# Eight more gate blocks in the mLSTM stage, between its heads, and two operations moved from POOL and DVE to ACT

## The chip, the cores and the metric

The kernel runs on one core of one Trainium2 chip. The metric is the device time of one execution in microseconds, the median over several runs. The engines are PE (matrix products), DVE (VectorE), ACT (ScalarE), POOL (GpSimd) and SP, which here only issues DMAs.

## The reference

One layer of a hybrid block over 512 latent tokens of width 1024 and 256 context tokens: a modulated norm, one wide projection, three branches (RWKV-7 with 8 heads, a depthwise convolution, mLSTM with 4 heads), a gated merge, and an MLP. Cut to what matters here:

```
h = rmsnorm(x, g_norm1) * (1 + mod_x[1]) + mod_x[0]
u_rw, u_cv, u_ml, u_gate = split(h @ w_in)        # u_gate: 3 x 1024 columns
ya = rwkv7(u_rw, context)                         # two directions, a scan over tokens
yc = mlstm(u_ml, context)                         # two directions, 4 heads
   hn = layernorm(h, nw);  return hn * sigmoid(o)
yb = silu(layernorm(depthwise_conv(a * sigmoid(g))))
ga, gb, gc = split(sigmoid(u_gate))
m = ga * (ya @ pa) + gb * (yb @ pb) + gc * (yc @ pc)
x = x + mod_x[2] * (m @ wo)
x = x + mod_x[5] * (square(relu(h2 @ w1)) @ w2);  return rmsnorm(x, g_final)
```

## The kernel before

All tokens stay on one core, features on the 128 partitions. Matrix products keep fp32 precision by splitting each operand into a high and a low part: a product of a 128 x 512 weight half takes three PE products (high by high, high by low, low by high). Each weight half is loaded by SP into `raw` (256 KB), ACT writes its high part `whi`, POOL its low part `wlo` (`whalf`, lines 156 to 160). A **dense block** of 128 output features takes two halves and 24 products of 128 x 128 by 128 x 512; its result lies in one of two PSUM banks (tag "d").

The stages, by time in the span: features of RWKV up to 300 us; the **mLSTM stage** from 300 to 531; four **weaves** of the RWKV scan, 531 to 620, 620 to 707, 707 to 793 and 793 to 870; the rest of the projections and the modulation vectors up to 948; then the merge and the MLP up to the end.

The mLSTM stage. `front(h)` computes a head's key, value, query and output gate by dense blocks (line 293), transposes them, and runs the state over its chunks: per chunk the key block is weighted on POOL into `kw` (line 836), PE multiplies it (`st`, line 838). `back(h)` computes the output: products `psc` and `acc`, a norm on DVE, four transposes into `pt` (line 889), and DVE's product into `yc` (line 891), stored to DRAM (line 892). Between the heads, DVE computes the convolution's taps (line 324), and the first RWKV pair's matrices are prepared: Gram products `pg` on PE (line 1006), a triangular inversion on DVE by rows (`N` and `tmp`, lines 1045 to 1052, `TN` 1055 and 1057), and its products `px` (lines 1066 to 1082). Last come the stage's gate blocks: dense products `dl`, tanh on ACT into `gt` (line 524), a store (line 525).

A weave runs one pair's scan: `chain` has 12 chunks of three steps each, S (line 1133), X (1139) and V (1148, with DVE's `SV`, 1149), where each step waits for ACT or DVE behind the step before. Between the steps, other work is issued: the next pair's matrices (`nxt`), and products of one stream `dense_`: gate blocks that the mLSTM stage left over (`gates()`, products `dg`, line 545), then the projections of two branches (`projections()`, products `dp`, line 624), which read the gates back (`ld`, line 619). `DENSE[j]` says how many products of the stream are paced evenly over the 36 steps of weave j, `EXTRA[j]` how many follow them. Weave 3 has in place of `nxt` the norm of the convolution branch (`conv_norm`) and the modulation sums (`wad` loads, DVE `accm`, line 641). What is left of the stream runs after the weaves.

The program is written in this order, and a scheduler places each instruction on its engine by its priority and modelled readiness; on the chip, each engine runs its list in order. A tile's tag and its number of buffers (`bufs`) say which earlier tile has to be done with.

Of the kernel before, what the change touches and what calls it, by code (L numbers as in the profile page):

```python
# [7 lines left out]
F32 = mybir.dt.float32  # L8
# [3 lines left out]
AF = mybir.ActivationFunctionType  # L12
# [5 lines left out]
P = 128  # L18
# [37 lines left out]
NRAW, NHI = 3, 4  # L56
NGA = 6
PART = (2, 4)
# [18 lines left out]
def build(tc, wblk, wada, xin, cin, params, lora, consts, rowp, out, dbg=None):  # L77
# [426 lines left out]
    for i, z, y in tiles:  # L504
        SY.dma_start(z, sp["z", i][:, :])
    st[0] = front(0)
    st[1] = front(1)
    back(0, *st[0])
    taps(tiles)
    for i, z, y in tiles:  # L510
# [3 lines left out]
    rw.open_a()  # L514
    rw.run(rw.ctx(0), rw.lat(0))
    st[2] = front(2)
    back(1, *st[1])
    st[3] = front(3)
    back(2, *st[2])
    back(3, *st[3])  # L520
    for g in range(NGA):
        ps, = dense(B_GA + g)
        t = SM.tile([P, NT], F32, tag="qT", name="gt", bufs=2)
        A.activation(t[:, :], ps[:, :], AF.Tanh, scale=0.5)
        SY.dma_start(sp["g", g][:, :], t[:, :])
    emm.close()
# [192 lines left out]
def mlstm(tc, nc, S, SG, PS1, dense, CN, C, ident, nwh, epsc, sp, sp_rows, dump, consts):  # L719
# [76 lines left out]
    def front(h):  # L796
# [13 lines left out]
        A.activation(to[:, :], pl[:, :], AF.Tanh, scale=0.5)  # L810
        G.tensor_scalar(to[:, :], to[:, :], 1.0, None, ALU.add)

# [11 lines left out]
        for d in range(2):  # L824
# [8 lines left out]
            for p in range(5):  # L833
                c = orders[d][p]
                kw = S.tile([P, 128], F32, tag="kw", name="kw", bufs=2)
                G.tensor_scalar(kw[:, :], ktok[:, c, :], cols[:, c, 2, rr:rr + 1], None, ALU.mult)
                st = PS1.tile([P, 129], F32, tag="tp", name="st", bufs=2)
                PE.matmul(st[:, :], lhsT=kw[:, :], rhs=v1[:, c, :], start=True, stop=True)
                if p == 0:
                    V.tensor_copy(cs[:, 0, :], st[:, :])  # L840
                else:
                    V.scalar_tensor_tensor(cs[:, p, :], cs[:, p - 1, :], wib[:, c * 128 + last:c * 128 + last + 1],
                                           st[:, :], ALU.mult, ALU.add)
# [3 lines left out]
    def back(h, qT, kT, to, v1, qs, Cst):  # L847
# [42 lines left out]
        yc = S.tile([P, NT], F32, tag="yc", name="yc")  # L890
        V.scalar_tensor_tensor(yc[:, :], pt[:, :], nwh[:, h:h + 1], to[:, :], ALU.mult, ALU.mult)
        SY.dma_start(sp["yc", h][:, :], yc[:, :])
# [4 lines left out]
PACE = [4] * 8 + [3] * 8 + [2] * 12 + [0] * 8  # L897
DENSE = (100, 100, 100, 110)
EXTRA = (20, 20, 20, 20)

# [621 lines left out]
```

## Time and profile before

| | |
|---|---|
| median of 3 runs | 1376.44 us (1365.84 to 1383.73) |
| profiled execution, its own time | 1368.34 us |
| its span | 1366.6 us |
| busy: PE | 1238.3 us (91%) |
| busy: DVE, ACT, POOL | 858.2, 511.2, 583.0 us |
| mean granted clock of PE | 0.955 |

Times in the rows are microseconds from the start of the span; ns where marked. A row of the windows gives the window, its length, then for PE, PEld (weight load), DVE, ACT and POOL the busy time with the number of instructions, then the granted clock of PE as a share of full speed, the busy share of the DMA engines, and GB/s. A row of a timeline gives start, length, engine, line, operation, output<-input, shapes, and in brackets the idle time before with what ended it. A row of the groups gives count, busy time, mean ns, and idle time before with its releasers. The chain of waits follows the work that ended last in a window back, and shares it out by line. Where many products follow each other, the distance of their starts tells their pace; their lengths overlap.

### The profile page before, as it was taken

Reading aid. Unit: us, or ns where it says so; the run is one execution under the profiler, and the core shown is the slowest. Engines: PE = TensorE matmul, PEld = TensorE weight load, DVE = VectorE, ACT = ScalarE, POOL = GpSimd, SP = SyncE. Lnnn points to the kernel's source line nnn. Section 1 sums busy time; section 2 is a strip of 40 time slices with the busy share of each in tenths; the row PEclk is TensorE's granted clock in tenths of the full one; section 3 lists DMA queues with packets and bytes.
Section 4 is the critical chain, followed back from the end, with each engine's and each line's share of the span. In section 5 each row is a group of like instructions: output and inputs, shape, how many; then the busy total and the mean of one; then the engine's idle time right before and its main releaser. Section 6 shows DMA issues by size and latency. Waiting matters only on the chain.

```text
span 1366.6 us, 21733 instructions
## 1 busy us (share of the span) xinstructions
PE 1238.3 (91%) x8020; PEld 964.7 (71%) x8020; DVE 858.2 (63%) x1513; ACT 511.2 (37%) x1048; POOL 583.0 (43%) x547
## 2 busy tenths in 40 slices
PE   5989989776999886998998888989999999999997
PEld 2678867565888675666676555667887878888886
DVE  5698788798357984796978957688284533300202
ACT  4426567432222221342443445322364333322222
POOL 1633434329554523332433454433465544444542
PEclk9999999888999998998999998999999999999999
DMA  9312688722622315241431254876444422432332
GB/s 375 99 58 63 197 264 245 229 75 70 200 78 91 125 53 150 85 131 60 136 117 48 86 164 146 275 247 234 139 131 142 136 93 93 154 101 95 129 98 87
DMA packets 101457, 187.85 MB, mean 137 GB/s; under 512 B 10708, under 2 KB 29396, under 8 KB 100328
## 3 DMA queue, kind: packets, MB, share of 16 engines
q1 hardware_dynamic: 101352, 186.47, 43.0%
q8 instruction: 63, 1.03, 0.3%
q14 instruction: 42, 0.34, 0.1%
HBM read 148.64 MB, written 29.40 MB: 130 GB/s over the span
## 4 chain that ended last, share of the span: by engine, by line
PE 42%; DVE 17%; DMA 6%; issue 2%; ACT 1%; POOL 0%; SPq 0%; DVEq 0%; ACTq 0%; POOLq 0%
PE pt L1301 16%; PE pd L1370 13%; DMA wad<-wada 5%; PE dg L545 4%; DVE N L1052 3%; DVE tmp L1050 3%; PE pg L1006 2%; DVE N L1045 2%; DVE accm L641 1%; PE pd L715 1%; DVE LT L1075 1%; PE ch L1133 1%; DVE SV L1149 1%; PE dl L293 1%; PE ch L1139 1%
## 5 line engine op out<-in xcount | busy, mean ns | idle before, releaser
L160 POOL TENSOR_TENSOR wlo<-raw,whi 128x512 fp32r<-128x512 f32 x296 | 430.8, 1461 | 554.8 <-ACT whi L159 496.3
L159 ACT CAST whi<-raw 128x512 fp32r<-128x512 f32 x296 | 181.7, 619 | 322.0 <-PE pt L1301 114.1
L293 PE MATMUL dl<-hh,whi 128*128 128x512 f32 (+1 forms) x344 | 143.2, 416 | 5.2 <-ACT kT L791 4.3
L293 PE MATMUL dl<-hh,wlo 128*128 128x512 f32 (+1 forms) x344 | 140.5, 408 | 0.0
L293 PE MATMUL dl<-hl,whi 128*128 128x512 f32 (+1 forms) x344 | 139.7, 406 | 0.0
L1370 PE MATMUL pd<-h2h,wlo 128*128 128x512 f32 (+1 forms) x272 | 105.2, 388 | 0.0
L1370 PE MATMUL pd<-h2l,whi 128*128 128x512 f32 (+1 forms) x272 | 104.5, 386 | 0.6 <-POOL h2l L1353 0.6
L1396 DVE TENSOR_TENSOR x<-pt,modb 128x512 f32<-128x512 f32 x8 | 5.5, 691 | 154.8 <-PE pt L1301 154.8
L1370 PE MATMUL pd<-h2h,whi 128*128 128x512 f32 (+1 forms) x272 | 102.3, 383 | 0.2 <-ACT h2h L1350 0.2
L1301 PE MATMUL pt<-whi,h1l 128*128 128x512 f32 x256 | 99.7, 389 | 0.0
L1301 PE MATMUL pt<-whi,h1h 128*128 128x512 f32 x256 | 99.7, 389 | 0.0
L1301 PE MATMUL pt<-wlo,h1h 128*128 128x512 f32 x256 | 99.2, 389 | 0.0
L293 PEld LDWEIGHTS dl<-hh,whi 128*128 128x128 f32 (+1 forms) x344 | 66.9, 194 | 20.4 <-ACT kT L791 4.5
L1374 DVE TENSOR_TENSOR relu<-relu 128x512 f32<-128x512 f32 x32 | 43.7, 1367 | 57.9 <-ACT relu L1373 57.8
L641 DVE SCALAR_TENSOR_TENSOR accm<-wad,scz,accm 128x512 f32<-128x512 f32 x56 | 57.6, 1028 | 34.2 <-DMA wad<-wada 33.6
L293 PEld LDWEIGHTS dl<-hh,wlo 128*128 128x128 f32 (+1 forms) x344 | 66.8, 194 | 14.3 <-issue 0.4
L293 PEld LDWEIGHTS dl<-hl,whi 128*128 128x128 f32 (+1 forms) x344 | 66.6, 194 | 13.8 <-issue 1.3
L1146 POOL TENSOR_TENSOR sps<-SV,PL 64x128 f32<-64x128 f32 x88 | 40.0, 454 | 78.6 <-DVE SV L1149 75.5
L545 PE MATMUL dg<-hl,whi 128*128 128x512 f32 x144 | 65.8, 457 | 0.0
L545 PE MATMUL dg<-hh,whi 128*128 128x512 f32 x144 | 65.0, 451 | 0.0
L545 PE MATMUL dg<-hh,wlo 128*128 128x512 f32 x144 | 64.9, 450 | 0.0
L1370 PEld LDWEIGHTS pd<-h2l,whi 128*128 128x128 f32 x272 | 51.7, 190 | 12.5 <-POOL h2l L1353 0.9
(399 smaller groups left out, 2824.7 us busy)
## 6 DMA issues: line engine op xcount, KB each, us to landing
raw<-wblk SPq DMA_DIRECT2D x296, 256.0 KB, 2.9
wad<-wada SPq DMA_DIRECT2D x64, 256.0 KB, 4.1
wada<-wada SPq DMA_DIRECT2D x8, 1024.0 KB, 12.0
BK<-kb SPq DMA_DIRECT2D x16, 384.0 KB, 5.1
sp_bk<-BK SPq DMA_DIRECT2D x8, 768.0 KB, 5.5
BK<-sp_bk SPq DMA_DIRECT2D x8, 768.0 KB, 4.2
sp_g<-gt SPq DMA_DIRECT2D x24, 256.0 KB, 2.0
sp_al<-al SPq DMA_DIRECT2D x8, 640.0 KB, 5.2
```

The source lines that it names most:

```text
L159: A.copy(hi[:, :], raw[:, :])
L160: G.tensor_tensor(lo[:, :], raw[:, :], hi[:, :], ALU.subtract)
L293: PE.matmul(ps_[0:M, :], lhsT=w[:, ko:ko + M], rhs=x[seg][:, k, :], start=(n == 0), stop=(n == 3 * KT - 1))
L545: yield lambda w=w, x=x, k=k, ko=ko, n=n: PE.matmul(ps[:, :], lhsT=w[:, ko:ko + P], rhs=x[:, k, :], start=(n == 0), stop=(n == 3 * KT - 1))
L641: V.scalar_tensor_tensor(o, t[:, :], sc[:, k, 0:1], o, ALU.mult, ALU.add)
L1006: PE.matmul(ps[hf, i, :, :], lhsT=BK[dd, c, x, :], rhs=al[:, c] if lat else AL[d][dd, 8 + c:9 + c, :], start=True, stop=True)
L1050: V.tensor_tensor(tv, N[:, s + 1:32, s:s + 1].to_broadcast([P, n, s]), N[:, s:s + 1, 0:s].to_broadcast([P, n, s]), ALU.mult)
L1052: V.tensor_tensor(N[:, s + 1:32, 0:s], N[:, s + 1:32, 0:s], tv, ALU.add)
L1146: last["Pool"] = G.tensor_tensor(sps[hf], SV[d][hf, c, :, :], PL[hf, c, :].unsqueeze(2).to_broadcast([64, 2, CH]), ALU.mult)
L1301: PE.matmul(pss[i][:, :], lhsT=x[:, k, ts_], rhs=w[:, :], start=(k == 0 and n == 0), stop=(k == nk - 1 and n == 2))
L1370: PE.matmul(ps[:, ts_], lhsT=w[:, ko:ko + P], rhs=x[:, k, ts_], start=(k == 0 and n == 0), stop=(k == 7 and n == 2))
L1374: V.tensor_tensor(t[:, :], t[:, :], t[:, :], ALU.mult)
```

## The change

Fourteen in place of six gate blocks are computed in the mLSTM stage, by calls of `gate(n)` between its heads, and what the weaves take of the stream falls from 120 to 64 products each in weaves 0 to 2, and rises from 130 to 140 in weave 3. The gate's result `gt` moves from two buffers of tag "qT" to the single buffer of tag "yc", which it shares with the heads' output. The key weighting `kw` goes from POOL to ACT; the output gate `to` is scaled and shifted on ACT, so that the last product of a head is a plain product on DVE.

```diff
--- before.py
+++ after.py
@@ -54,7 +54,7 @@
     _o += _c
 NCONST = _o
 NRAW, NHI = 3, 4
-NGA = 6
+NGA = 14
 PART = (2, 4)
 
 
@@ -503,9 +503,22 @@
     tiles = [(i, CZ.tile([P, 752], F32, name=f"cz{i}")[:, :], CZ.tile([P, NT], F32, name=f"cy{i}")[:, :]) for i in (2, 3)]
     for i, z, y in tiles:
         SY.dma_start(z, sp["z", i][:, :])
+
+    left = iter(range(NGA))
+
+    def gate(n):
+        for _, g in zip(range(n), left):
+            ps, = dense(B_GA + g)
+            t = SM.tile([P, NT], F32, tag="yc", name="gt")
+            A.activation(t[:, :], ps[:, :], AF.Tanh, scale=0.5)
+            SY.dma_start(sp["g", g][:, :], t[:, :])
+
     st[0] = front(0)
+    gate(1)
     st[1] = front(1)
+    gate(1)
     back(0, *st[0])
+    gate(2)
     taps(tiles)
     for i, z, y in tiles:
         SY.dma_start(sp["yb", i][:, :], y)
@@ -513,16 +526,17 @@
     rw = Rwkv(tc, CN, C, ident, epsc, PL, sp, dump)
     rw.open_a()
     rw.run(rw.ctx(0), rw.lat(0))
+    gate(1)
     st[2] = front(2)
+    gate(2)
     back(1, *st[1])
+    gate(1)
     st[3] = front(3)
+    gate(2)
     back(2, *st[2])
+    gate(1)
     back(3, *st[3])
-    for g in range(NGA):
-        ps, = dense(B_GA + g)
-        t = SM.tile([P, NT], F32, tag="qT", name="gt", bufs=2)
-        A.activation(t[:, :], ps[:, :], AF.Tanh, scale=0.5)
-        SY.dma_start(sp["g", g][:, :], t[:, :])
+    gate(NGA)
     emm.close()
     ew.close()
     ehc.close()
@@ -808,7 +822,7 @@
         to = S.tile([P, NT], F32, tag="to", name="to", bufs=2)
         pl, = dense(B_ML + 12 + h)
         A.activation(to[:, :], pl[:, :], AF.Tanh, scale=0.5)
-        G.tensor_scalar(to[:, :], to[:, :], 1.0, None, ALU.add)
+        A.activation(to[:, :], to[:, :], AF.Identity, scale=nwh[:, h:h + 1], bias=nwh[:, h:h + 1])
 
         v1 = S.tile([P, 6, 129], F32, tag="v1", name="v1", bufs=2)
         G.memset(v1[:, :, 128:129], 1.0)
@@ -833,7 +847,7 @@
             for p in range(5):
                 c = orders[d][p]
                 kw = S.tile([P, 128], F32, tag="kw", name="kw", bufs=2)
-                G.tensor_scalar(kw[:, :], ktok[:, c, :], cols[:, c, 2, rr:rr + 1], None, ALU.mult)
+                A.activation(kw[:, :], ktok[:, c, :], AF.Copy, scale=cols[:, c, 2, rr:rr + 1])
                 st = PS1.tile([P, 129], F32, tag="tp", name="st", bufs=2)
                 PE.matmul(st[:, :], lhsT=kw[:, :], rhs=v1[:, c, :], start=True, stop=True)
                 if p == 0:
@@ -888,15 +902,15 @@
             V.tensor_scalar(ht[:, c, :], ht[:, c, :], mv[:, c, 0:1], rstd[:, c:c + 1], ALU.subtract, ALU.mult)
             PE.transpose(pt[:, c * 128:(c + 1) * 128], ht[:, c, :], ident)
         yc = S.tile([P, NT], F32, tag="yc", name="yc")
-        V.scalar_tensor_tensor(yc[:, :], pt[:, :], nwh[:, h:h + 1], to[:, :], ALU.mult, ALU.mult)
+        V.tensor_tensor(yc[:, :], pt[:, :], to[:, :], ALU.mult)
         SY.dma_start(sp["yc", h][:, :], yc[:, :])
 
     return front, back
 
 
 PACE = [4] * 8 + [3] * 8 + [2] * 12 + [0] * 8
-DENSE = (100, 100, 100, 110)
-EXTRA = (20, 20, 20, 20)
+DENSE = (54, 54, 54, 120)
+EXTRA = (10, 10, 10, 20)
 
 
 class Rwkv:
```

The functions after it move by 14 lines: `dg` is line 559 there, the chain's steps are 1147, 1153 and 1162, `gt` of the stage is line 513 and its store 514, the heads' store 906.

SP at the end of the mLSTM stage (`sp_g`: store of a gate; `sp_yc`: store of a head's output; `raw`: a weight half; `ld`: a gate read back; `SV`: the first load of weave 0). Before:

```order
L525 DMA sp_g_128<-gt 128x512
L156 DMA raw<-wblk 128x512 x2
L525 DMA sp_g_129<-gt 128x512
L156 DMA raw<-wblk 128x512 x3
L892 DMA sp_yc_116<-yc 128x512
L1100 DMA SV_4802<-sp_v_93 64x4x128
```

With the change:

```order
L514 DMA sp_g_134<-gt 128x512
L906 DMA sp_yc_116<-yc 128x512
L514 DMA sp_g_135<-gt 128x512
L514 DMA sp_g_136<-gt 128x512
L156 DMA raw<-wblk 128x512 x2
L514 DMA sp_g_137<-gt 128x512
L633 DMA ld<-sp_g_132 128x512
L633 DMA ld<-sp_g_133 128x512
L1114 DMA SV_5122<-sp_v_93 64x4x128
```

Three gate stores now stand behind the last head's store, and they and two reads ahead of weave 0's first load.

PE at a step of weave 0 (`hh`, `hl`: the high and low part of the tokens; `ch`: the chain's products). Before:

```order
L545 MATMUL dg<-hh_169,whi 128x512
L545 MATMUL dg<-hl_171,whi 128x512
L545 MATMUL dg<-hh_169,wlo 128x512
L1139 MATMUL ch_6182<-xc_6202,LT_4789 64x64 x2
L1139 MATMUL ch_6183<-xc_6206,LT_4789 64x64 x2
L545 MATMUL dg<-hh_169,whi 128x512
L545 MATMUL dg<-hl_171,whi 128x512
L1148 MATMUL ch_6182<-UV_4799,BKt_4797 64x64
```

With the change:

```order
L559 MATMUL dg<-hh_169,wlo 128x512
L559 MATMUL dg<-hh_169,whi 128x512
L1153 MATMUL ch_6306<-xc_6325,LT_5109 64x64 x2
L1153 MATMUL ch_6307<-xc_6329,LT_5109 64x64 x2
L559 MATMUL dg<-hl_171,whi 128x512
L1162 MATMUL ch_6306<-UV_5119,BKt_5117 64x64
```

Between two steps of the chain stand one or two products in place of two or three.

PE in the second half of weave 3. Before:

```order
L1133 MATMUL ch_8273<-SV_4803,AL_4795 64x64
L545 MATMUL dg<-hl_171,whi 128x512
L545 MATMUL dg<-hh_169,wlo 128x512
L545 MATMUL dg<-hh_169,whi 128x512
L1139 MATMUL ch_8272<-xc_8284,LT_4789 64x64 x2
L1139 MATMUL ch_8273<-xc_8288,LT_4789 64x64 x2
L545 MATMUL dg<-hl_171,whi 128x512
```

With the change:

```order
L1162 MATMUL ch_8235<-UV_5120,BKt_5118 64x64
L1147 MATMUL ch_8286<-SV_5122,AL_5111 64x64
L1147 MATMUL ch_8286<-SV_5122,AL_5114 64x64
L1147 MATMUL ch_8287<-SV_5123,AL_5112 64x64
L1147 MATMUL ch_8287<-SV_5123,AL_5115 64x64
L613 MATMUL cr<-cst,rsq 128x128 x4
L1153 MATMUL ch_8286<-xc_8309,LT_5109 64x64 x2
L1153 MATMUL ch_8287<-xc_8313,LT_5109 64x64 x2
```

The gate products of weave 3 have run out by then, and some nine steps of the chain stand with no product of the stream among them.

## Rows read from the trace of the kernel before

**Rows 1.** Windows of the span, all engines: window, its length, engines, granted clock, DMA.

```profile
300.00:339.00 39.00, 27.49 (x150) 23.35 (x151) 34.17 (x49) 12.27 (x23) 29.38 (x11) 0.88 0.23 76
...
441.00:489.00 48.00, 41.65 (x216) 34.82 (x215) 45.52 (x119) 13.43 (x25) 24.52 (x22) 0.96 0.33 108
489.00:532.00 43.00, 29.66 (x317) 24.60 (x318) 27.11 (x75) 8.43 (x16) 10.34 (x15) 0.83 0.27 84
532.00:620.00 88.00, 80.90 (x927) 57.47 (x928) 68.56 (x128) 30.59 (x93) 29.14 (x43) 0.91 0.45 131
620.00:707.00 87.00, 79.25 (x934) 56.06 (x930) 70.99 (x141) 32.85 (x96) 29.43 (x41) 0.92 0.29 86
707.00:793.00 86.00, 77.92 (x894) 54.39 (x892) 70.23 (x136) 33.53 (x98) 31.62 (x41) 0.98 0.29 88
793.00:870.00 77.00, 66.39 (x487) 44.52 (x486) 48.90 (x96) 34.58 (x93) 43.41 (x43) 0.89 0.59 180
```

**Rows 2.** The same for products of line 293, one window.

```profile
489.00:532.00 43.00, 17.90 (x65) 12.52 (x65) 0.83 0.27 84
```

**Rows 3.** Timeline of PE, two spots: start, length, instruction.

```profile
506.08 0.63 PE L293 MATMUL dl<-hh,whi 128*128 128x512 f32 x1
506.51 0.63 PE L293 MATMUL dl<-hl,whi 128*128 128x512 f32 x1
...
507.55 0.39 PE L293 MATMUL dl<-hl,whi 128*128 128x512 f32 x1
507.78 0.40 PE L293 MATMUL dl<-hh,wlo 128*128 128x512 f32 x1
```

**Rows 4.** Chain of waits by line, weaves 0 to 2 and weave 3.

```profile
by line: PE dg L545 18.8%; PE pg L1006 13.2%; DVE tmp L1050 12.3%; DVE N L1052 10.7%; DVE LT L1075 6.8%; issue 5.5%; PE ch L1139 4.0%; DVE SV L1149 3.6%; PE pbk L1031 3.3%; PE ch L1133 3.3%; PE ch L1148 2.9%; DVE N L1045 2.8%; PE px L1082 2
by line: PE dg L545 15.1%; DVE N L1052 13.7%; PE pg L1006 11.6%; DVE tmp L1050 10.4%; issue 6.7%; DVE N L1045 6.3%; DVE SV L1149 3.4%; DVE AL L1017 3.4%; PE pbk L1031 3.3%; PE ch L1133 3.2%; PE ch L1139 2.9%; DVE LT L1009 2.5%; DVE TN L1055
by line: PE dg L545 16.9%; DVE N L1052 14.0%; PE pg L1006 10.0%; DVE tmp L1050 9.9%; issue 7.2%; DVE N L1045 6.5%; SPq L570 3.8%; PE ch L1133 3.6%; PE ch L1139 3.2%; DVE SV L1149 3.2%; DVE AL L1017 2.5%; DVE TN L1055 2.4%; PE pbk L1031 2.3%
by line: DMA wad<-wada 44.3%; DVE accm L641 8.7%; PE dg L545 8.6%; issue 8.1%; DMA yld<-sp_yc 5.6%; DVE macc L583 3.2%; PE ch L1148 3.1%; DVE SV L1149 2.8%; PE pmr L665 2.7%; SPq L570 2.3%; PE pm L1243 2.2%; PE ch L1139 2.0%; PE ch L1133 1.
```

**Rows 5.** Waits of PE, 339 to 532: total, times, longest.

```profile
PE st L838 <- POOL kw L836: 10.8, 1, 10.8
```

**Rows 6.** Timeline of POOL around 321 to 341.

```profile
321.25 15.40 POOL L160 TENSOR_TENSOR wlo<-raw,whi 128x512 fp32r<-128x512 f32 x2 [3.38 <-ACT whi L159]
...
338.12 1.18 POOL L836 TENSOR_SCALAR kw<-ktok,cols 128x128 f32<-128x128 f32 x2
```

**Rows 7.** Timeline of DVE in the same stretch.

```profile
319.66 14.65 DVE L324 SCALAR_TENSOR_TENSOR cy<-cz,dwh,cy 128x512 f32<-128x512 f32 x22
```

**Rows 8.** Timeline of DVE around 451.

```profile
450.57 0.27 DVE L1052 TENSOR_TENSOR N<-N,tmp 128x108 f32<-128x108 f32 x1
451.20 1.43 DVE L1052 TENSOR_TENSOR N<-N,tmp 128x130 f32<-128x130 f32 x1
```

**Rows 9.** Timeline of POOL around 451.

```profile
451.19 1.29 POOL L160 TENSOR_TENSOR wlo<-raw,whi 128x512 fp32r<-128x512 f32 x1 [2.47 <-ACT whi L159]
```

**Rows 10.** Timeline of all engines, last transposes to the first chain.

```profile
525.98 1.16 PE L889 MATMUL pt<-cst,ht 128*128 128x128 f32 x4 [6.18 <-DVE ht L888]
527.17 0.75 DVE L891 SCALAR_TENSOR_TENSOR yc<-pt,dv,to 128x512 f32<-128x512 f32 x1 [0.57 <-PE pt L889]
527.95 0.33 SPq L892 DMA_DIRECT2D sp_yc<-yc  x1
...
531.34 1.35 PE L1133 MATMUL ch<-SV,AL 128*64 128x64 f32 x8 [4.21 <-DMA SV<-sp_v]
```

**Rows 11.** Groups by line, 300 to 532: busy, mean ns, idle before.

```profile
L822 ACT COPY ktok<-tp 128x384 f32<-128x384 f32 x8 | 3.7, 478 | 5.3 <-PE tp L821 5.2
...
L524 ACT ACTIVATE gt<-dl 128x512 f32<-128x512 f32 x6 | 3.6, 595 | 17.2 <-issue 10.2 <-PE dl L293 6.9
```

**Rows 12.** DMA issues, 300 to 532: KB, us to landing.

```profile
sp_yc<-yc SPq DMA_DIRECT2D x4, 256.0 KB, 2.0
```

## The prediction

> **What bounds the kernel now.** I read the windows first, since the shares over the whole span hide that the stages have different limits. From the window of the mLSTM stage on, see who is busy: PE for 41.7 of 48 us in 441 to 489 with DVE at 45.5, PE for 29.7 of 43 us in 489 to 532, PE for 78 to 81 and DVE for 69 to 71 of the 86 to 88 us of weaves 0 to 2 [rows 1]. So these stages are neither full on PE nor on DVE: work of both alternates with waits. The granted clock falls there too: 0.83 in 489 to 532, 0.91, 0.92 and 0.98 in the weaves, 0.89 in weave 3. The two levels are 2.4 and 1.2 GHz, so a mean of 0.91 over 88 us is 15.8 us at the lower one; weaves 0 to 2 together have 15.8 + 13.9 + 3.4 = 33 us of it.
>
> Next the pace of a dense product: 0.23 us from start to start at the upper level, 0.43 at the lower, which the engine still had after a pause [rows 3]. Then the chain of waits of each weave: gate products hold 18.8%, 15.1% and 16.9% of it, DVE's inversion (N, tmp) as much again and more [rows 4]. In weave 3 the chain is 44.3% the loads of the modulation weights [rows 4]. Last, the single waits of the mLSTM stage: PE stood 10.8 us for one `kw` [rows 5].
>
> **The change part by part.** The profiled execution took 1368.3 us, 8.1 below the median of the runs; the sum is made against it.
>
> *Eight gate blocks into the mLSTM stage.* 8 x 24 = 192 products at 0.227 us are 43.6 us of PE. What of it lies in time that PE now waits?
>
> Up to the last Gram product of that stage PE's list holds 67 products more: 15.2 us. The large gap there is the 10.8 us for `kw` [rows 5]. Its cause is on POOL: two `wlo` took 15.4 us, from 321.25 to 336.65, while DVE ran 22 taps without pause in 319.66 to 334.31; `kw` stood behind them [rows 6, 7]. With `kw` on ACT the wait for POOL is gone from `kw`; but the product that comes next needs the `wlo` that is late, and with a gate block on either side there is one more `wlo` to be made in that stretch. So I take only 3 of the 10.8 us as gained, with bounds 0 and 10.8, another 3 for waits that gate products fill, and 3 for small products that move behind: +6 us (0 to +15).
>
> In 441 to 489 DVE is busy 45.5 of 48 us [rows 1]: what PE gets there is free, and `wlo` more or less beside DVE moves it by a microsecond. −1 (−3 to +3).
>
> From the first `px` to weave 0's first chain product PE has 195 dense products in place of 65 [rows 2]. The stretch was some 42 us (489 to 531); 65 products at pace would be 14.8 us, and the rest was small products, waits and the lower clock. 130 more are 29.5 us. Against it: the waits for `TN` and for head outputs that they fill, I take 5 us of the 13.3 in which PE is not busy in that window [rows 1], because the longest of them, 6.2 us before the last transposes [rows 10], still has no product in front of it in the new order; and some 2 us of lower clock returned, out of 43 x 2 x 0.17 = 14.6 us at that level. With the tail it is more: behind the last transposes there was 0.75 us of `yc` and 4.2 us in all until the chain's first product [rows 10]. Now three gates share the one "yc" buffer with the last head's output. The last transposes end, `yc` 0.75, its issue 0.33, its store 2.0 [rows 10, 12], only then `gt` 0.6 [rows 11], which frees the PSUM bank for the last gate's 24 products, 5.5, then `gt` 0.6, three issues of 0.33 on SP (its store and two reads), 3.1 until SV lands (the wait of 4.2 less `yc` and issue): 13.9 us, 9.7 more than before, of which 5.5 are the products already counted. +29.5 − 5 − 2 + 4.2 = +27 (+15 to +34).
>
> Stage: 6 − 1 + 27 = **+32 us** (+12 to +46; the whole 43.6 and the tail's 4.2 less a little is the upper end).
>
> *`kw` and `to` on ACT, `yc` on DVE.* ACT is busy 12 to 13 of 39 and 48 us there [rows 1], a `kw` on POOL took 0.59 us [rows 6], and the nearest ACT rows are 0.48 for 384 columns and 0.60 for 512 [rows 11]; 40 at 0.25 to 0.5 are 10 to 20 us on an engine that is idle for more than twice that. What they can do is stand behind a gate's tanh or a weight cast on ACT. Nothing on the path, −2 to +3, inside the bounds above. A plain product for `yc` is 0.75 at most: 0.
>
> *Weaves 0 to 2.* 56 products off 120 in each. On the chain their share was 18.8% of 89, 15.1% of 86 and 16.9% of 85: 16.7 + 13.0 + 14.4 = 44.1 us [rows 4]; 56/120 of it is −20.6. Each weave loses 4.7 `wlo`. One beside DVE costs a row of the inversion 1.16 us (1.43 for 0.27) [rows 8, 9]; 14 of them, at half that because not each meets such a row and half of the chain is elsewhere, would be −6 to −8, of which −3 on the chain. Against it: fewer products leave PE idle more often between the steps, and its clock then stands at 1.2 GHz for longer; +2. **−22** (−10 to −36: above, the lower clock doubles; below, each weave is DVE's 69 to 71 us and a few more, 12 off each).
>
> The Trainium skill ("SBUF — State Buffer", "SBUF: two separate sides") says that DVE and GpSimd share a port pair as an exclusive lock: whoever starts first holds it for the whole instruction, and the other blocks. By that rule, 14 casts of 1.29 us would be 18 us of DVE given back, for the −6 to −8 above, if each met DVE at work. The rows agree in the single case [rows 8, 9], but the two `wlo` that stood 15.4 us beside a row of taps [rows 6, 7] show that POOL can lose the pair for many instructions, so the price is not one instruction a time.
>
> *Weave 3 and the rest of the stream.* The modulation loads hold 44.3% of the chain there, gate products 8.6% [rows 4]; the new order has nine chain steps without a product and puts 65 products behind them, where 34 fewer are left for after the chain. The loads go on at their pace: −2 (−8 to +8). Beyond, nothing moves: 0.
>
> Sum: 32 − 22 − 2 = +8, say +8 to +9: 1368.3 + 8.7 = **1377 us**, which against the median of the runs is no change.
>
> **The rivals.**
>
> *Forecast*, stage +32, weaves −22, 0.55: 1377, its own range 1362 to 1392.
>
> *The clock takes it back*, 0.10. Weaves 0 to 2 stood 33 us at 1.2 GHz with 120 products [rows 1]; with 64 they stand 65 us there, the small products on the chain (`pg`, `pbk`, `ch`, some 20% of it) run at half pace and the weaves give 10 us in place of 22: 1389. For it speaks 0.83 in the window with the sparsest products, against it 0.98 in weave 2 where they are as dense as in weave 0. The Trainium skill ("TensorE: Matmul & The Clock Gate", "What's actually happening") has it that "the default state is throttled, and activity releases the throttle"; the 0.43 pace after a pause [rows 3] agrees with the rule.
>
> *Slower*, 0.12: the gates fill nothing. They sit in the stage as solid runs of 24 products, ahead of the small ones that DVE waits for, so each run delays DVE by its 5.5 us; and one "yc" buffer with two PSUM banks holds PE at each store of 2.0 us [rows 12]. Stage +46, weaves −10: 1368 + 36 = 1404. It decides from the point where less than 5 us of the 31 us in which PE was idle in the windows at 300, 441 and 489 [rows 1] is filled. Against it: the blocks are spread between heads, and only the tail shows the store in the path.
>
> *Faster*, 0.23: the weaves fall to DVE's floor, 88, 87 and 86 to 75 each, −36, and the stage hides 20 of its 43.6 us (+24), because `kw` on ACT takes the whole of the 10.8 us off: 1368 − 14 to 1368 − 30 where wait and clock in the stage go as well: 1338 to 1354, 1346 in the middle. For it: DVE at 79 to 82% of the weaves is the next limit, and the chain through gate products is all that stands above it. Against: DVE's idle time in a weave lies at its start, where it waits for Gram products, which the change doesn't shorten.
>
> That the change doesn't do what it says is not a case of its own: the order shows the blocks between the heads, except for the 24 products behind the last transposes, which are in the sum.
>
> **How the numbers follow.** The runs shown lie within ±9 us of their median, and 2% of 1376.4 is 27.5 us: faster is under 1349, slower over 1404. The forecast and the clock rival lie within; of the slower rival about half is beyond 1404 (0.06), and of the faster one seven in ten below 1349 (0.16); the spread of the forecast adds 0.04 to each side. Faster 0.20, within 0.70, slower 0.10. The range leaves out one in ten at each end, and so reaches into both of these: 1344 to 1403.
>
> **What would show it.** Windows of the changed profile: the mLSTM stage (300 to the first chain product) about 263 us long, for 231; weaves 0 to 2 about 239 us in sum, for 261. If their chain still holds 15% of gate products, or DVE's N and tmp rise to fill the time, the weave term fails. PE's wait for `kw` should be gone, and a wait of the products for `wlo` or for weights stand in its place. Behind the last transposes, about 14 us until SV. Their clock under 0.85 would show the clock rival. A gain over 27 us, or stage time within 15 us of before, would make the prediction wrong.

## The result and the profile after

The changed kernel takes 1447.93 us (median of 4, 1444.61 to 1450.01), the kernel before 1371.62 us (median of 4). The ratio is 1.054, with a 95% interval of 1.046 to 1.063: 5.4% slower, 45 us above the top of the predicted range. The mean granted clock of PE over the span fell from 0.955 to 0.894. The windows in this document are those of one profiled execution of each kernel, and the runs of one kernel spread by 3 to 18 us, so a few microseconds between two stages are not read as an effect on their own.

I split both spans at the first chain product of weave 0, at the first X product of weave 3 (the first that needs the matrices prepared for weave 3), and at the end of weave 3's last X product, so that the stages of the two kernels answer to each other. The windows of the kernel before (window, length, busy time and instructions of PE, PEld, DVE, ACT, POOL, granted clock, DMA share, GB/s):

```profile
300.00:531.30 231.30, 198.49 (x1373) 167.86 (x1373) 162.05 (x410) 59.11 (x110) 119.63 (x108) 0.93 0.33 103
531.30:793.00 261.70, 238.74 (x2747) 168.43 (x2747) 209.77 (x404) 96.96 (x285) 90.20 (x125) 0.94 0.34 102
793.00:871.40 78.40, 67.80 (x499) 45.37 (x498) 49.32 (x97) 34.58 (x93) 43.41 (x43) 0.89 0.59 183
871.40:1366.60 495.20, 477.10 (x2145) 386.25 (x2143) 195.74 (x267) 168.68 (x311) 220.15 (x168) 0.99 0.43 139
```

The same of the changed kernel:

```profile
300.00:577.60 277.60, 243.13 (x1565) 204.55 (x1565) 155.77 (x408) 87.85 (x177) 108.57 (x79) 0.93 0.35 108
577.60:873.50 295.90, 262.18 (x2591) 187.09 (x2591) 200.12 (x404) 86.07 (x267) 74.46 (x114) 0.68 0.25 72
873.50:956.80 83.30, 67.72 (x496) 46.61 (x495) 56.82 (x105) 35.63 (x95) 41.99 (x43) 0.86 0.62 197
956.80:1447.30 490.50, 471.07 (x2111) 382.43 (x2109) 188.25 (x258) 164.88 (x304) 218.54 (x165) 0.98 0.42 134
```

Length by length: the mLSTM stage +46.3 us, weaves 0 to 2 +34.2, weave 3 +4.9, the rest −4.7. The sum is 80.7 us, the whole difference of the spans (1447.3 to 1366.6). The second row has the surprise. Weaves 0 to 2 lost 168 dense products by the pacing numbers, and became longer. DVE did the same 404 instructions there, in 200.1 us for 209.8, but PE's granted clock fell from 0.94 to 0.68: at two levels of 1.2 and 2.4 GHz, 261.7 x 2 x 0.06 = 31 us at the lower one before, 295.9 x 2 x 0.32 = 189 us after. The gate products alone in this window (window, length, busy time and instructions of PE and PEld, granted clock, DMA), before and after:

```profile
531.30:793.00 261.70, 118.70 (x350) 60.60 (x350) 0.94 0.34 102
577.60:873.50 295.90, 93.11 (x195) 40.81 (x195) 0.68 0.25 72
```

So PE has 155 gate products fewer there and is busy 23 us longer (262.2 for 238.7), which only slower products can do; it is idle for 33.7 us in place of 23.0.

The expectations further down were written with another split: weave 3 begins at its first S product in the kernel before (783.3), and a chunk later, at its second S step, in the changed kernel (876.3). Counted so, weaves 0 to 2 take 252.0 and 298.7 us, and weave 3 87.7 and 80.1. These windows do not hold the same work, as the products `px` of line 1081 (1095 with the change) show in the two windows of weaves 0 to 2:

```profile
L1081 PE MATMUL px<-LT,TN 32*32 32x32 f32 x96 | 4.6, 213 | 1.1 <-DVE LT L1075 1.1
L1095 PE MATMUL px<-LT,TN 32*32 32x32 f32 x144 | 9.5, 237 | 5.0 <-DVE LT L1089 5.0
```

A third of them falls into weave 3 before, and none after. The sizes that the expectations start from are too far apart by this, and the gain in weave 3 that they speak of is not one. All windows below are split as above.

The chain of waits in weaves 0 and 1 after the change, by line (line 559 is the gate product, 1020 the Gram product), answers to the first two rows of [rows 4]:

```profile
by line: PE pg L1020 18.3%; PE dg L559 18.2%; PE ch L1147 8.3%; DVE N L1059 7.0%; DVE LT L1089 6.1%; DVE tmp L1064 5.4%; PE ch L1162 4.8%; PE ch L1153 4.4%; PE pbk L1045 4.1%; DVE N L1066 3.9%; issue 3.0%; DVE AL L1031 2.2%; DVE TN L1069 2.
by line: PE pg L1020 18.7%; PE dg L559 13.8%; DVE LT L1089 6.5%; PE ch L1153 5.5%; DVE N L1066 5.4%; PE pbk L1045 5.2%; issue 5.2%; PE ch L1147 4.9%; DVE tmp L1064 4.0%; PE ch L1162 4.0%; DVE N L1059 2.9%; DVE SV L1163 2.8%; DVE TN L1069 2.
```

Gate products kept 18.2% and 13.8%, with about half as many of them; the Gram products went from 13.2% and 11.6% to 18.3% and 18.7%, DVE's inversion down. The chain has moved from DVE to PE. One line of PE in weaves 0 to 2 shows it best. The 576 Gram products, which the change does not touch, in the kernel before (count, busy time, mean ns, idle time before):

```profile
L1006 PE MATMUL pg<-AL,BK 64*64 64x128 f32 (+1 forms) x576 | 37.8, 270 | 5.6 <-DVE AL L1017 5.6
```

and in the changed kernel:

```profile
L1020 PE MATMUL pg<-AL,BK 64*64 64x128 f32 (+1 forms) x576 | 60.4, 381 | 6.2 <-DVE AL L1031 6.2
```

The same 576 products are busy 60.4 us in place of 37.8.

In the mLSTM stage PE's granted clock is 0.93 in both kernels. PE is busy 44.6 us longer there (243.1 for 198.5) and idle 34.5 us for 32.8: on balance the added products filled no idle time. The waits of PE there after the change (total, times, longest), first up to 442 us, then from 500 to the end:

```profile
PE dl L293 <- POOL wlo L160: 11.2, 1, 11.2
...
PE ch L1147 <- DMA SV<-sp_v: 5.8, 1, 5.8
PE pt L903 <- DVE ht L902: 5.1, 1, 5.1
PE dl L293 <- ACT gt L513: 3.6, 1, 3.6
```

The 10.8 us that PE waited for `kw` [rows 5] is gone, and 11.2 us of a product for its `wlo` stands in its place. The 6.2 us before the last transposes [rows 10] became 5.1, and a wait of 3.6 us behind them is new.

### The profile page after: what moved, and what is told of

It is laid out like the page before. It is cut to its first block, busy times and chain, and to the rows that moved or that the text cites. A ratio compares the mean times of both kernels' runs of the same rounds, so it can differ in the third digit from the quotient of the medians.

```text
span 1447.3 us, 21724 instructions
## 1 busy us (share of the span) xinstructions
PE 1302.4 (90%) x8020; PEld 1019.1 (70%) x8020; DVE 842.4 (58%) x1513; ACT 526.4 (36%) x1092; POOL 552.2 (38%) x503
## 4 chain that ended last, share of the span: by engine, by line
PE 55%; DVE 16%; DMA 8%; issue 3%; POOL 2%; ACT 2%; SPq 0%; DVEq 0%; ACTq 0%; POOLq 0%
PE pt L1315 15%; PE pd L1384 12%; PE dl L293 8%; PE pg L1020 4%; DMA wad<-wada 4%; PE dg L559 3%; DVE N L1066 2%; PE pd L729 2%; POOL wlo L160 2%; DVE tmp L1064 2%; DVE N L1059 2%; PE ch L1147 1%; DVE LT L1089 1%; DVE cy L324 1%; PE ch L1153 1%
## 5 line engine op out<-in xcount | busy, mean ns | idle before, releaser
L293 PE MATMUL dl<-hh,whi 128*128 128x512 f32 (+1 forms) x408 | 168.8, 414 | 10.1 <-ACT gt L513 5.4
L293 PE MATMUL dl<-hh,wlo 128*128 128x512 f32 (+1 forms) x408 | 165.3, 405 | 11.2 <-POOL wlo L160 11.2
L293 PE MATMUL dl<-hl,whi 128*128 128x512 f32 (+1 forms) x408 | 164.2, 402 | 0.0
L1384 PE MATMUL pd<-h2h,wlo 128*128 128x512 f32 (+1 forms) x272 | 105.0, 387 | 0.0
L293 PEld LDWEIGHTS dl<-hh,whi 128*128 128x128 f32 (+1 forms) x408 | 79.1, 194 | 28.7 <-ACT gt L513 5.9
L293 PEld LDWEIGHTS dl<-hh,wlo 128*128 128x128 f32 (+1 forms) x408 | 78.7, 193 | 28.6 <-POOL wlo L160 11.7
L293 PEld LDWEIGHTS dl<-hl,whi 128*128 128x128 f32 (+1 forms) x408 | 78.9, 193 | 16.4 <-issue 1.3
L1020 PE MATMUL pg<-AL,BK 64*64 64x128 f32 (+1 forms) x768 | 73.7, 356 | 8.5 <-DVE AL L1031 6.2
L1020 PEld LDWEIGHTS pg<-AL,BK 64*64 64x64 f32 x768 | 57.0, 196 | 27.9 <-issue 22.0
L655 DVE SCALAR_TENSOR_TENSOR accm<-wad,scz,accm 128x512 f32<-128x512 f32 x56 | 51.5, 920 | 32.0 <-DMA wad<-wada 31.5
L1023 DVE TENSOR_TENSOR LT<-pg,cst 64x256 f32<-64x256 f32 x48 | 20.2, 421 | 83.6 <-PE pg L1020 83.4
```

The lines of the kernel that those rows point to most:

```text
L293: PE.matmul(ps_[0:M, :], lhsT=w[:, ko:ko + M], rhs=x[seg][:, k, :], start=(n == 0), stop=(n == 3 * KT - 1))
L655: V.scalar_tensor_tensor(o, t[:, :], sc[:, k, 0:1], o, ALU.mult, ALU.add)
L1020: PE.matmul(ps[hf, i, :, :], lhsT=BK[dd, c, x, :], rhs=al[:, c] if lat else AL[d][dd, 8 + c:9 + c, :], start=True, stop=True)
L1384: PE.matmul(ps[:, ts_], lhsT=w[:, ko:ko + P], rhs=x[:, k, ts_], start=(k == 0 and n == 0), stop=(k == 7 and n == 2))
```

## Experiments

Theory A, formed from the second rows of the two tables: products of the gates keep PE's clock up between the steps of the chain; with half of them gone the clock falls, and the small products on the chain run at half pace. In the mLSTM stage the added products are paid in full. Rivals: ScalarE's new work delays the heads (B); the weaves do shorten, and something else was lost (C, D, G).

**The engines alone.** The kernel before with the three changed operations (the code here and below is shortened).

```diff
-G.tensor_scalar(kw, ktok[c], cols[c], None, ALU.mult)
+A.activation(kw, ktok[c], AF.Copy, scale=cols[c])
-G.tensor_scalar(to, to, 1.0, None, ALU.add)
+A.activation(to, to, AF.Identity, scale=nwh[h], bias=nwh[h])
-V.scalar_tensor_tensor(yc, pt, nwh[h], to, ALU.mult, ALU.mult)
+V.tensor_tensor(yc, pt, to, ALU.mult)
```

> The kernel before with only the three operations moved (key weighting and output gate on ScalarE, plain product for the head's output); gates and pacing as before. Theory A (the loss of the change comes from the PE clock in the weaves and from the added products in the mLSTM stage): within 6 us of before, 1366 to 1378, weaves 0 to 2 within 5 us of 252 in sum, about 34 us of them at the lower clock. Theory B (the ScalarE work delays the heads): 1385 or more, the mLSTM stage 15 us longer than 231.

Measured: 1367.72 us, ratio 0.996 (0.994 to 0.999). The windows of the stage and of weaves 0 to 2:

```profile
300.00:526.90 226.90, 197.76 (x1369) 167.85 (x1369) 162.63 (x408) 74.70 (x154) 88.91 (x64) 0.93 0.34 105
526.90:788.40 261.50, 238.62 (x2747) 168.60 (x2747) 208.10 (x404) 97.52 (x285) 90.12 (x125) 0.93 0.34 102
```

and PE's longest waits up to 441 us:

```profile
PE dl L293 <- POOL wlo L160: 6.3, 1, 6.3
PE st L838 <- ACT kw L836: 2.8, 1, 2.8
```

B falls. The stage is 4.4 us shorter, the weaves stay as they were (261.5 us for 261.7). In place of 10.8 us for `kw` PE waits 6.3 us for a `wlo` and 2.8 for `kw`: the `wlo` that is made beside the row of taps is still late, and once `kw` no longer stands behind it on POOL, a dense product waits for it.

**The pacing alone.** The kernel before with the two rows of numbers; of the 168 products that weaves 0 to 2 give up, weave 3 takes 10 and 158 run after the chain.

```diff
-DENSE = (100, 100, 100, 110)
-EXTRA = (20, 20, 20, 20)
+DENSE = (54, 54, 54, 120)
+EXTRA = (10, 10, 10, 20)
```

> The kernel before with only the two rows of pacing numbers of the change; six gates in the mLSTM stage, so that 168 products more run after the weaves. Theory A (clock): weaves 0 to 2 become longer, not shorter: from 252 us to 290 to 305, with 150 us or more at the lower clock; total 1371 + 45 + 38 (168 products at 0.227) = 1450 within 15. Theory C (what was predicted: weaves shorten by 7 us each with 56 products fewer): weaves 230, total 1371 - 22 + 38 = 1387.

Measured: 1431.67 us, ratio 1.044 (1.040 to 1.048). Weaves 0 to 2, weave 3, the rest:

```profile
530.20:808.40 278.20, 237.84 (x2588) 171.23 (x2588) 201.09 (x404) 85.36 (x264) 75.94 (x114) 0.75 0.29 85
808.40:890.00 81.60, 69.41 (x508) 46.29 (x507) 53.05 (x101) 32.35 (x89) 33.73 (x36) 0.86 0.46 139
890.00:1423.50 533.50, 515.91 (x2293) 417.64 (x2293) 191.03 (x262) 182.73 (x335) 242.76 (x186) 0.99 0.44 140
```

With the mLSTM stage as before, fewer products make weaves 0 to 2 16.5 us longer (278.2 for 261.7), with 278.2 x 2 x 0.25 = 139 us at the lower clock. C asked for 22 us less and falls. A's direction holds, but its size, 38 to 53 us more, was at least twice too high; the rest pays the products put there in full (+38.3, where 158 x 0.227 would be 35.9).

**More work in the weaves.** The changed kernel, with each gate product of weaves 0 to 2 issued twice.

```diff
+for r in range(R):                     # R = 2 for the gates of weaves 0 to 2
-    yield lambda ...: PE.matmul(ps, lhsT=w, rhs=x, start=(n == 0), ...)
+    yield lambda ...: PE.matmul(ps, lhsT=w, rhs=x, start=(n == 0 and r == 0), ...)
-A.activation(t, ps, AF.Tanh, scale=0.5)
+A.activation(t, ps, AF.Tanh, scale=0.5 / R)
-DENSE = (54, 54, 54, 120); EXTRA = (10, 10, 10, 20)
+DENSE = (108, 108, 108, 120); EXTRA = (20, 20, 20, 20)
```

> The changed kernel, with each of its gate products in weaves 0 to 2 issued twice into the same sum and the gate's scale halved: the same results, 192 products more on PE, in the weaves alone. Theory A (clock): more work makes it faster: weaves 0 to 2 from 299 us back to 250 to 270, under 60 us of them at the lower clock, total 1400 to 1420. Theory D (the weaves are longer for another reason, the order of the chain's products or the loads): 192 x 0.227 = 44 us are added, total 1475 to 1495, the lower clock as before.

Measured: 1417.32 us, ratio to before 1.034 (1.029 to 1.039), 31 us faster than the changed kernel although PE does 192 products more. The stage and weaves 0 to 2:

```profile
300.00:577.20 277.20, 246.66 (x1563) 207.47 (x1562) 154.88 (x408) 87.71 (x177) 108.59 (x79) 0.92 0.35 108
577.20:839.90 262.70, 238.78 (x2783) 172.15 (x2783) 201.38 (x404) 85.83 (x265) 75.39 (x115) 0.93 0.28 82
```

The Gram products in those weaves (line 1023 here):

```profile
L1023 PE MATMUL pg<-AL,BK 64*64 64x128 f32 (+1 forms) x576 | 36.6, 269 | 2.9 <-DVE AL L1034 2.9
```

The stage is the changed kernel's, 277 us. The weaves fall from 295.9 to 262.7 us, the length before the change (261.7), the clock rises from 0.68 to 0.93, and the Gram products are back to 269 ns from 381. D, by which 44 us would be added, falls. The order is not held still by this run: the scheduler places the instructions anew for each kernel (the last `px` of weave 3's matrices ends 6 us before weave 3's first S product in the changed kernel, at 863.98 for 870.16, and 8 us behind it in this one, at 839.99 for 832.45). But an order alone would not take PE's busy time from 262.2 to 238.8 us with 192 products more; products that run faster do. The Trainium skill ("TensorE: Matmul & The Clock Gate", "What's actually happening") says that "the default state is throttled, and activity releases the throttle"; by that rule repeated products can pay for themselves, and these rows agree (0.68 to 0.93).

**The gates at the end.** The changed kernel with all fourteen gates behind the last head, in two buffers.

```diff
-    gate(1)   ...   gate(2)            # the calls between the heads
 ...
     gate(NGA)
-            t = SM.tile([P, NT], F32, tag="yc", name="gt")
+            t = SM.tile([P, NT], F32, tag="qT", name="gt", bufs=2)
```

> The changed kernel with all fourteen gates behind the last head, in the two qT buffers as before the change. Theory E (between the heads the gates filled no wait, the stage grew by all of their 43.6 us): within 8 us of the changed kernel, 1440 to 1456, the mLSTM stage 272 to 285 us long. Theory F (they filled 10 us or more, and something else in the stage was lost): stage 288 or longer, total 1458 or more. If the one shared buffer costs as much as its two waits at the stage's end, 3.8 and 5.9 us, the stage is 5 to 8 us shorter.

Measured: 1427.94 us, ratio 1.042 (1.037 to 1.046): 20 us faster than the changed kernel, and faster than E or F had it. The stage and weaves 0 to 2:

```profile
300.00:570.30 270.30, 242.20 (x1566) 204.78 (x1567) 166.53 (x411) 88.61 (x177) 108.58 (x79) 0.95 0.36 111
570.30:851.10 280.80, 249.12 (x2587) 176.51 (x2587) 200.97 (x404) 86.04 (x265) 76.76 (x115) 0.72 0.29 85
```

The stage is 7.3 us shorter than with the gates between the heads. Against the kernel with the engines alone (226.9 us) it is +43.4: 192 x 0.227 = 43.6 us, paid in full. So the gates between the heads hid nothing, and their placing and the shared buffer together cost 7 us more; that this is the size expected for the buffer does not show that it was the buffer, since both were changed here. A larger part of the gain, 15.1 us, comes from weaves 0 to 2, 280.8 for 295.9 us, in which the two kernels have the same work.

**The same products in two weaves.** The changed kernel, 96 products each in weaves 0 and 1, none paced into weave 2.

```diff
-DENSE = (54, 54, 54, 120); EXTRA = (10, 10, 10, 20)
+DENSE = (86, 86, 0, 120); EXTRA = (10, 10, 0, 20)
```

> The changed kernel with the same 192 products of weaves 0 to 2 in another place: 96 each in weaves 0 and 1, none paced into weave 2. Theory A (the PE clock follows how much PE has to do between the chain's steps): weaves 0 and 1 back to 90 us or less each with under 30 us at the lower clock, weave 2 over 95 us with 75 us or more at it, total 1425 to 1445. Theory G (the changed kernel's weaves are slow by how their work is ordered or by what the mLSTM stage leaves behind, whatever the products): all three stay at 95 to 104 us, total 1448.

Measured: 1430.68 us, ratio 1.043 (1.040 to 1.046). Weaves 0, 1 and 2, each up to the first X product of the next:

```profile
580.50:667.00 86.50, 74.72 (x918) 52.69 (x918) 68.02 (x128) 29.78 (x91) 27.64 (x42) 0.91 0.44 128
667.00:763.30 96.30, 85.25 (x859) 60.29 (x857) 70.32 (x140) 29.87 (x90) 26.37 (x39) 0.77 0.21 64
763.30:849.20 85.90, 63.06 (x820) 50.91 (x818) 63.90 (x136) 27.33 (x86) 20.72 (x33) 0.69 0.18 51
```

Weave 0, with 98 gate products in its window, is back (86.5 us, 0.91; 98.8 us at 0.67 in the changed kernel), which speaks against G. Weave 1, with 79, is not (96.3 us, 0.77), and weave 2, with 18, is short at 0.69 (85.9 us; 105.0 in the changed kernel). Theory A missed both: a weave at a low clock is not long where PE has little to do in it (busy 63.1 of 85.9 us). Together the three take 268.7 us for 295.9, with the same number of products: where they stand counts as well as how many they are.

**Two buffers in the tail.** The changed kernel; the last three gates use the two qT buffers.

```diff
-    gate(NGA)
+    gate(NGA, "qT", 2)                 # tag and bufs of the gate's tile
```

> The changed kernel, but the last three gates of the mLSTM stage in the two qT buffers, which no head needs any more by then, in place of the one buffer shared with the head's output. Theory H (the shared buffer is what the tail costs): the waits of 3.8 us behind the last transposes and of 5.3 us before them are gone, the stage 6 to 9 us shorter, 269 to 272, total 1438 to 1443. Theory I (the tail is bound by the 24 products and the loads of the scan's states): within 2 us of 277 us.

Measured: 1433.95 us, ratio 1.046 (1.043 to 1.049). The stage and weaves 0 to 2:

```profile
300.00:575.50 275.50, 243.16 (x1566) 204.98 (x1567) 159.28 (x411) 88.64 (x178) 109.91 (x80) 0.92 0.35 112
575.50:856.20 280.70, 249.75 (x2587) 177.38 (x2587) 201.20 (x404) 85.13 (x264) 75.05 (x114) 0.71 0.28 82
```

PE's waits from 500 us to the end of the stage:

```profile
PE pt L903 <- DVE ht L902: 7.0, 2, 6.3
PE ch L1147 <- DMA SV<-sp_v: 5.0, 1, 5.0
```

The wait of 3.6 us behind the transposes is gone, but the wait in front of them (6.3) and that for SV (5.0) stay, and the stage gains 2.1 us only, as theory I had it. Weaves 0 to 2, whose work was not touched, are again 15.2 us shorter (280.7), which is all that the kernel gained (14 us).

**Fewer gates in the stage.** The way back: four gates, and two, with the engines as changed.

```diff
-NGA = 6
-DENSE = (100, 100, 100, 110)
+NGA = 4                                # or 2
+DENSE = (100, 100, 100, 100)           # with two gates (116, 116, 116, 100)
```

> The other way: the ScalarE operations of the change, but four gates in the mLSTM stage in place of six; weaves 0 to 2 keep their 120 products, weave 3 has gate products alone. Theory A (products in the weaves keep the clock up and are partly free, products in the mLSTM stage are not): stage 227 - 11 = 216 us, weaves 0 to 2 within 4 us of 252, weave 3 from 90 to 75 to 80 us as it doesn't wait for the convolution's norm, the rest 6 us longer: 1367 - 11 - 12 + 6 = 1350. Theory J (the weaves pay whatever the stage saves): 1362 to 1370.

> The same with two gates in the mLSTM stage and 136 products in each of weaves 0 to 2. Theory A: stage 205 us, the 16 products more a weave (3.6 us) half hidden, lower clock under 30 us in weaves 0 to 2 together: 5 us faster than with four gates, 1345. Theory J (weaves are full with 120): as with four gates or up to 5 us slower.

Measured: four gates 1380.65 us, ratio 1.005 (1.002 to 1.008); two gates 1390.90, ratio 1.013 (1.010 to 1.017). The stage and the rest with four gates:

```profile
300.00:525.40 225.40, 190.88 (x1330) 162.39 (x1329) 164.71 (x414) 71.78 (x148) 84.16 (x60) 0.92 0.32 99
...
863.70:1380.40 516.70, 495.80 (x2200) 400.94 (x2200) 202.04 (x266) 175.19 (x323) 233.73 (x178) 0.98 0.43 140
```

and with two the stage, weaves 0 to 2, and weave 2 alone:

```profile
300.00:514.60 214.60, 179.61 (x1277) 152.83 (x1278) 158.48 (x409) 68.15 (x142) 78.58 (x56) 0.89 0.31 96
514.60:797.50 282.90, 256.33 (x2798) 184.19 (x2798) 209.38 (x404) 99.90 (x291) 95.47 (x130) 0.89 0.33 99
694.80:797.50 102.70, 89.80 (x898) 64.60 (x897) 69.76 (x136) 34.16 (x99) 31.90 (x42) 0.82 0.24 72
```

Both are slower than the engines alone, against A and J alike. Against the engines alone, with four gates the stage saved 1.5 us, not 11, weave 3 (75.8 for 81.3) 5.5, and the rest pays 22.5 us for 57 products more. With two, the stage saves 12.3 us, but weaves 0 to 2 grow by 21.4 with 48 products more (10.9 us at 0.227), weave 3 is about the same (80.1), and the rest is 17.4 longer. Beyond 120 a weave the products cost more there than in the stage. And more of them did not keep the clock up: weave 2 stands at 0.82 with them (102.7 us), where it had 0.98 before. Theory A has no reason for that.

**Seven gates, weave 3 as in the changed kernel.** With the engines as changed.

```diff
-NGA = 6
-DENSE = (100, 100, 100, 110)
+NGA = 7
+DENSE = (100, 100, 100, 120)
```

> ScalarE operations of the change, seven gates at the end of the mLSTM stage, weaves 0 to 2 with their 120 products as before, and weave 3 and what follows as in the changed kernel (48 gate products, 140 in all). Theory K (the 7 us of weave 3 and 5 us of what follows that the changed kernel won come from weave 3's own products, whatever the weaves before it hold): stage 227 + 5.5 = 232 us, weave 3 80 to 83, the rest 491: 1368 + 5 - 8 - 4 = 1361, a little faster than with the ScalarE operations alone. Theory J (what one place saves another pays): 1368 to 1374.

Measured: 1382.30 us, ratio 1.008 (1.005 to 1.011). Weave 3 and the rest:

```profile
799.30:890.70 91.40, 73.76 (x509) 49.91 (x508) 58.47 (x107) 36.27 (x97) 47.78 (x44) 0.85 0.58 183
890.70:1383.40 492.70, 473.58 (x2111) 384.02 (x2109) 185.34 (x257) 164.99 (x304) 220.63 (x165) 0.98 0.42 133
```

Theory K falls, and with the split used here it had nothing to explain: weave 3 is not shorter in the changed kernel (83.3 us for 78.4). Against the engines alone the stage is up 7.4 us (234.3), weaves 0 to 2 are 3.5 longer (265.0), weave 3 takes 91.4 us for 81.3, and the rest is at 492.7 for 494.2. With the same products of the stream weave 3 is 8.1 us longer here than in the changed kernel; why is open.

**Ten gates at the end.** Half of the move, with the engines as changed.

```diff
-NGA = 6
-DENSE = (100, 100, 100, 110); EXTRA = (20, 20, 20, 20)
+NGA = 10
+DENSE = (80, 80, 80, 120); EXTRA = (16, 16, 16, 20)
```

> Half of the move: ten gates, all at the end of the mLSTM stage, 96 products in each of weaves 0 to 2 (120 before, 64 with the change), weave 3 as in the changed kernel. Theory A (clock, by degrees): stage 227 + 22 = 249, weaves 0 to 2 together 252 to 275 with 60 to 120 us at the lower clock, total 1385 to 1405. Theory L (the clock is lost only near 64 products): weaves 240 to 250, under 45 us at the lower clock, total 1370 to 1380.

Measured: 1414.27 us, ratio 1.028 (1.022 to 1.034). The stage and weaves 0 to 2:

```profile
300.00:546.10 246.10, 221.16 (x1469) 187.05 (x1470) 166.37 (x411) 81.53 (x165) 98.01 (x70) 0.93 0.35 108
546.10:839.00 292.90, 270.55 (x2687) 189.22 (x2687) 207.76 (x404) 92.42 (x277) 86.45 (x123) 0.75 0.28 86
```

L falls. With 96 products a weave the weaves are nearly as long as with 64 in the changed kernel (292.9 us, 292.9 x 2 x 0.25 = 146 us at the lower clock), and longer than in the other kernels with 64 (278 to 281); A had the direction and, with up to 23 us more than before for 31.2 measured, put the size 8 us or more too low.

## Why the prediction was wrong, step by step

**Weaves 0 to 2, −22 us: the step that failed.** They took +34.2. The step multiplied the gate products' share of the chain by 56/120, and put the clock at +2 us. It was 189 us at the lower clock in place of 31. The pacing alone shows the sign without the rest of the change (+16.5), and the doubled products turn it round (262.7 us at 0.93). At the lower clock the products that are left, the Gram products above all, take over the chain that gate products and DVE held. One part of the term did come: with fewer `wlo` beside it DVE needed 9.7 us less for its 404 instructions (200.1 for 209.8), near the 6 to 8 that were reckoned, but the time was no longer on its chain.

**The rival that had it** was the clock, at 0.10. Its mechanism, and its sign that the clock would fall under 0.85, are what the runs show; its size was not: I took 65 us at the lower clock and 10 us of saving left. The argument against it in the prediction, that weave 2 had 0.98 with the same products, read one weave with 120 products as if it said something on 64.

**The mLSTM stage, +32 (bounds +12 to +46).** +46.3, at the upper end of the bounds. Three reductions in that sum did not come. The first, 3 us off the wait for `kw`, fell through the `wlo`: POOL's weight casts beside the taps, in the changed kernel

```profile
320.57 17.76 POOL L160 TENSOR_TENSOR wlo<-raw,whi 128x512 fp32r<-128x512 f32 x3 [3.38 <-ACT whi L159]
```

and DVE's taps there

```profile
318.98 16.98 DVE L324 SCALAR_TENSOR_TENSOR cy<-cz,dwh,cy 128x512 f32<-128x512 f32 x24
```

are three casts in 17.8 us beside 24 taps in 17.0; the product behind them is late by 11.2 us. That limit was seen in the prediction [rows 6, 7], and still too much was taken off for it. On ACT `kw` itself cost what was assumed, 0.40 us:

```profile
L850 ACT ACTIVATE kw<-ktok,cols 128x128 f32<-128x128 f32 x40 | 14.6, 399 | 16.9 <-PE st L852 16.8
```

The second, 5 us of waits to be filled late in the stage, left the largest where it was (5.1 of 6.2). The third is the tail. PE, from the last transposes to weave 0's first chain product:

```profile
559.22 1.16 PE L903 MATMUL pt<-cst,ht 128*128 128x128 f32 x4 [5.10 <-DVE ht L902]
...
565.39 0.63 PE L293 MATMUL dl<-hh,whi 128*128 128x512 f32 x1
565.82 0.63 PE L293 MATMUL dl<-hl,whi 128*128 128x512 f32 x1
...
569.32 0.39 PE L293 MATMUL dl<-hh,wlo 128*128 128x512 f32 x1
569.55 0.39 PE L293 MATMUL dl<-hh,whi 128*128 128x512 f32 x1
...
577.56 0.66 PE L1147 MATMUL ch<-SV,AL 128*64 128x64 f32 x4 [5.82 <-DMA SV<-sp_v]
```

and ACT's first gate behind it, which waited for the store:

```profile
563.29 0.60 ACT L513 ACTIVATE gt<-dl 128x512 f32<-128x512 f32 x1 [18.61 <-DMA sp_yc<-yc]
```

From the end of the transposes (559.22 + 1.16 = 560.38) to the chain's first product (577.56) are 17.2 us, for 13.9 predicted and 4.2 before. The store of `yc` delays the first gate to 563.29 as reckoned; but the last gate's products then start after a wait, ten of them at a pace of 0.43 us, that of the lower clock (565.39, 565.82), and only then at 0.23 (569.32, 569.55), and the wait behind them for SV is 5.8 us. The two-buffer run shows that the buffer was not the tail's price (2.1 us): without its wait the one in front of the transposes stayed. With the gates at the end, the added products cost 43.4 us over the engines alone: none was hidden. What their placing between the heads and the shared buffer added to that, 7.3 us, is measured only as a sum.

**Engines, −2 to +3.** −4.4 us of the stage, and 0.4% of the kernel: a little better than the bounds, and the only part of the change that pays.

**Weave 3 and the rest, −2 (bounds −8 to +8).** +4.9 and −4.7, together nothing, within the bounds. That 34 products fewer are left for the end would be −7.7 us at 0.227, of which 4.7 came.

**The slower rival** (stage +46, weaves −10, 1404) had the stage, in its size and in its reason that the gates fill nothing, and the wrong sign in the weaves; the faster one needed weaves at DVE's floor (78 to 82% of the weaves before by [rows 1], not 79), and DVE is busy 200 to 202 us there in the kernels with 192 products, of 269 to 296 us.

What is shown and what is not: the five kernels with 192 products in weaves 0 to 2 all stand at a lower clock there than the kernels with 360 or with doubled products (0.92 to 0.94), and thinning alone and doubling give the sign either way. What sets the size is not settled. With the same 192 products evenly spread the weaves took 278.2, 280.7, 280.8 and 295.9 us in four kernels, with 0.75, 0.71, 0.72 and 0.68, and neither the 96 products a weave of the ten gates nor the 136 of the two gates fit a rule by number. So about half of the 34.2 us goes with the thinning in every kernel, and what the changed kernel loses beyond that is open. The scheduler's order, which is made anew for each kernel, was held still in none of these.

Of all kernels the engines alone is the best: 1367.72 us, 0.996 of before (0.994 to 0.999), 0.945 of the changed kernel by the medians.

## What to carry to other kernels

Before moving matrix products away from a stage where they run between short dependent steps, look at the granted clock there: they may be what keeps it up, and then their removal lengthens every product that stays. A share of the chain of waits says what work was last, not what the time would be without it; where the granted clock already falls now and then, test the removal alone and a doubling of what is left, since those two give the sign at the price of two runs. Split two kernels at an instruction that needs the same work done in both: one chunk of the chain in the split moved 12 us from one stage to the next here, and made a gain in weave 3 that was none. Work moved into a stage costs its whole length until a named wait with its releaser has been shown to take it.

## What the runs showed of the hardware

More products made a kernel faster: 192 repeated ones, 44 us of work at full pace, took 31 us off. A small product of 64 by 64 on a thinly used PE took 381 ns in the mean, 269 ns with the repeated products beside it. ACT weights a 128 x 128 block in 0.40 us where POOL took 0.59 [rows 6], and POOL's weight cast beside an unbroken row of DVE's taps took about six microseconds (three in 17.8), 1.29 without the taps [rows 9].
